# Four attention heads whose probabilities are turned by VectorE and a DRAM round trip and not by TensorE

## The chip, the cores and the metric

The kernel runs on one core of a Trainium2 chip. Its time is the device time of one execution in microseconds; before the change the median of three runs is 907.01 us (906.93 to 907.70). All data are fp32; most matrix products split each fp32 operand into a rounded high part and a rest ("h" and "l") and add three products of the parts.

## The reference

One layer on x of 512 tokens by 1024 features: a SwiGLU feed-forward block, a token mixer, a second feed-forward block and a norm. The mixer has four differential heads (the ones that change here) and eight dilated heads, which the kernel takes in four pairs. For a differential head the reference computes, cut to what matters:

```python
# q, k: two maps (m = 0, 1) of 64 features per head; v: 128 features per head
s = einsum('bhmqd,bhmkd->bhmqk', q, k) * scale + bias      # causal: -inf where k > q
p = softmax(s, axis=-1)
a = p[:, :, 0] - lam * p[:, :, 1]                           # 512 x 512, lower triangle
o = einsum('bhqk,bhkd->bhqd', a, v)
oa = rmsnorm(o, subln_gain) * (1 - lam0)                    # norm over the 128 features of a head
mixed = concatenate([oa, ob]); x = x + mixed @ w_out        # ob: the dilated heads
```

## The kernel before

The mixer is written as a list of chunks for TensorE (PE). Chunk t belongs to step t: function `step` first calls what was `put` at that step with a rank below 10, in order of rank, then the chunk, then what has a rank of 10 and more. PE, VectorE (DVE) and ScalarE (ACT) execute in exactly this written order; the queues that issue DMAs, SyncE's (SP) and GpSimd's, are put in order by the planner of the framework. So a chunk's neighbours on PE, DVE and ACT are known from the numbers in `put`, and DMA issues may be moved among each other.

The chunks are: the projections q and k of units 0 and 1, the values of all units, then eight chunks for q and k of each of the units 2 to 7 (steps 44 to 91, six products of 512 columns a chunk), then the output projection `wo` (from step 92). Units 0 to 3 are the differential heads, 4 to 7 the dilated pairs. A head's attention starts at a step s (41, 49, 57 and 65 for the differential heads): it rides between the projection chunks of later units.

A differential head before the change, `attention(u, s)`:

- `score(m, i)` (L1736 to L1742), one a step from s to s+7: for a block of 128 queries i and map m, two products give up to (i+1) x 128 scores in a PSUM bank (two such banks in turn), DVE adds the bias and takes the row's extreme (L1739), ACT takes the exponential and its sum (L1742). The result lies in the tile `pr` of its map.
- `combine(i)` (L1746 to L1752): DVE joins the two maps, p0 + c p1, in place of p0. Ten blocks of 128 x 128 are left, with queries on the partitions.
- `turn` (L1879, L1881): the value product needs the keys on the partitions. PE turns each of the ten blocks against the identity into a PSUM bank and ACT copies the bank to `ptx`, in three groups of four, two and four blocks.
- `values` (L1891), at s+13: for every block a product with the turned block as stationary operand (128 x 128) and 128 columns of v as moving operand; the framework issues two instructions for each.
- `squares`, `mean`, `scale`, `finish`, `finish_low` (L1897 to L1935), one to seven steps after that: ACT squares with row sums, POOL's power for the norm, `scale` (L1915) in one DVE instruction of 512 columns, four transposes on PE (L1921), ACT and DVE write the two parts `mh` and `ml` that `wo` reads.

The dilated units 5 and 6 already have another way for part of their blocks: `flip` (L1766) turns 32 x 32 squares within a tile on DVE, `away` (L1772) writes the tile to DRAM in four DMAs so that the squares come into place, `back` (L1783) reads it in one DMA, and `values_moved` (L1808) uses it as the moving operand. The tile `tx` holds the turned blocks of all units (one buffer of 3072 columns). Unit 6 turns its other half on PE, `turn_rows` (L1793, L1794).

```python
step, tv = 2 if u else 1, s + 13
put(tv - 2 - step, 2, turn, ((0, 2), (1,)))
put(tv - 2, 2, turn, ((3,),))
put(tv, 1, values)
e = tv + 1
```

Line 188, 189 and 190 are the three products of `mm3`, which the projections, the feed-forward blocks and `wo` use.

Of the kernel before, what the change touches and what calls it, by code (L numbers as in the profile page):

```python
# [28 lines left out]
NQ = S // P  # L29
# [7 lines left out]
WARM = 8  # L37
DIRECT = (7,)
MOVED = {5: (0, 1), 6: (1,)}
PAIRED_ROWS = 5  # L40
BACK = {5: 7, 6: 9}
TAKEN = {5: 16, 6: 13}


# [71 lines left out]
HS = S // 2  # L116
# [11 lines left out]
def tile_macaron(ctx: ExitStack, tc, xs, xT, wf, wgu1, wst1, wdg1, wqk, wvd, wo, wgu2, wst2,  # L128
                 wdg2, fg, lams, relb, addc, xn, out):
    nc = tc.nc  # L130
    V, A, G, T = nc.vector, nc.scalar, nc.gpsimd, nc.tensor
# [4 lines left out]
    tp = ctx.enter_context(tc.tile_pool(name="tp", bufs=2))  # L136
# [3 lines left out]
    dp = ctx.enter_context(tc.tile_pool(name="dp", bufs=1, space=DRAM))  # L140
# [5 lines left out]
    def mm_bank(nm):  # L146
        return pp.tile([P, S], F32, tag="mm", name=nm, bufs=4)
# [10 lines left out]
    x = [None] + [cp.tile([P, S], F32, tag=f"x{k}", name=f"x{k}")[:] for k in range(1, KD)]  # L158
# [930 lines left out]
    with tc.manual_schedule(engines={mybir.EngineType.DVE, mybir.EngineType.Activation}):  # L1089
        for t in range(4):  # L1090
            raw = wp.tile([P, 1024], F32, tag="raw", name=f"raw_f{t}")
            h, l = w_place()
            for kk in range(2):
                k = 2 * t + kk
                c = slice(kk * 512, kk * 512 + 512)
# [282 lines left out]
    start = {w: 8 * i + 20 * (i > 2) for i, w in enumerate(plan)}  # L1378
# [5 lines left out]
    def put(t, rank, f, *a):  # L1384
        at.setdefault(t, []).append((rank, f, a))

    units, chunks = [], []
# [46 lines left out]
    vt = {}  # L1434
# [275 lines left out]
    def attention(u, s):  # L1710
        diff, quick, moved = u < 4, u == 7, u in MOVED
        st = {}
        order = (1, 2, 0, 3) if u >= PAIRED_ROWS else range(NQ)

        def row(m, i):
            w = (i + 1) * P
            if u < PAIRED_ROWS:
                return st["pr"][m][:, OFF[i]:OFF[i] + w]
            o = m * 640 + (0, 0, 2 * P, P)[i]
            return st["pr"][i in (1, 2)][:, o:o + w]  # L1720
# [47 lines left out]
        def away(n):  # L1768
            st["pd", n] = d = dp.tile([4, 32, 4, 320], F32, tag=f"pd{n}", name=f"pd{u}{n}")
            for r in range(4):  # L1770
                part = slice(32 * r, 32 * r + 32)
                nc.sync.dma_start(d[:].rearrange("c j r e -> r j c e")[r],  # L1772
                                           st["tr", n][part, :].rearrange("p (c e) -> p c e", c=4))

        def turned_tx():
            if not shared_tx:
                shared_tx.append(tp.tile([P, 12 * HS], F32, tag="tx", name="ptx_dilated", bufs=1))
            return shared_tx[0]

        def back(n):  # L1780
            o = n * 1280
            st["x", n] = turned_tx()[:, o:o + 1280]
            nc.sync.dma_start(st["x", n], st["pd", n][:].rearrange("c j r e -> (c j) (r e)"))  # L1783

        def turn_rows(part):

            tx = st["x", 0] = turned_tx()[:, :1280]
            pt = pp.tile([P, S], F32, tag="t", name=f"pt{u}{part[0][0]}{part[0][1]}", bufs=2)
            n = 0
            for m, i in part:  # L1790
                o = m * 640 + (0 if i == 0 else P)
                for k in range(i + 1):
                    T.transpose(pt[:, n + k * P:n + (k + 1) * P], row(m, i)[:, k * P:(k + 1) * P], ident[:])  # L1793
                A.copy(tx[:, o:o + (i + 1) * P], pt[:, n:n + (i + 1) * P])  # L1794
                n += (i + 1) * P

        def values_moved():
            po = st["po"] = mm_bank(f"po{u}")
# [19 lines left out]
        def turn_part(m, part):  # L1818


            pt = pp.tile([P, S], F32, tag="t", name=f"pt{u}{m}{part[0][0]}", bufs=2)
            n = 0
            for k, i0, i1 in part:
                for i in range(i0, i1):
                    T.transpose(pt[:, n:n + P], row(m, i)[:, k * P:(k + 1) * P], ident[:])
                    n += P

            if "tx" not in st:
                st["tx"] = turned_tx()
                st["used"] = 0  # L1830
            if quick:

                tx = st["tx"][:, m * KEYS[NQ]:(m + 1) * KEYS[NQ]]
                if part[0][1] == NQ - 1:
                    o = KEYS[1] - P
                    A.copy(tx[:, o:o + 2 * (KEYS[2] - KEYS[1])]
                           .rearrange("p (k q) -> p k q", k=2)[:, :, :P],
                           pt[:, :2 * P].rearrange("p (k q) -> p k q", k=2))
                    A.copy(tx[:, KEYS[NQ] - 2 * P:], pt[:, 2 * P:])
                    return  # L1840
                n = 0
                for k, i0, i1 in part:
# [4 lines left out]
            ptb = st["tx"][:, st["used"]:st["used"] + n]  # L1847
            st["used"] += n
            A.copy(ptb[:, :n], pt[:, :n])
            st["ptb", m, part] = ptb  # L1850

# [17 lines left out]
        def turn(tiles):  # L1869

            if "tx" not in st:
                st["tx"] = tp.tile([P, 12 * HS], F32, tag="tx", name=f"ptx{u}", bufs=1)
            for own in tiles:
                pt = pp.tile([P, S], F32, tag="t", name=f"pt{u}{own[0]}", bufs=2)
                n, c0 = 0, st.get("used", 0)
                for i in own:
                    st["place", i] = c0 + n
                    for k in range(i + 1):
                        T.transpose(pt[:, n:n + P], row(0, i)[:, k * P:(k + 1) * P], ident[:])  # L1879
                        n += P  # L1880
                A.copy(st["tx"][:, c0:c0 + n], pt[:, :n])  # L1881
                st["used"] = c0 + n
# [29 lines left out]
        def scale():  # L1912
            po3, ob = st["po3"], st["ob"]
            V.tensor_tensor(st["f2"], st["f2"], st["y"][:], op=ALU.mult)
            V.tensor_tensor(ob, po3, st["f"][:].to_broadcast([P, NQ, P]), op=ALU.mult)  # L1915

        def finish():
            if diff:
# [24 lines left out]
        step = 1 if quick else 2  # L1943
# [5 lines left out]
                6.5 if (n == 2 if u > 3 and not quick else u == 0 and n == 3) else 5, combine, i)  # L1949
        if diff:  # L1950

            step, tv = 2 if u else 1, s + 13
            put(tv - 2 - step, 2, turn, ((0, 2), (1,)))
            put(tv - 2, 2, turn, ((3,),))
            put(tv, 1, values)
            e = tv + 1
            put(e, 7, squares)
            put(e + 1, 7, mean)
            put(e + 4, 7, scale)
            put(e + 6, 3, finish)  # L1960
            put(e + 7, 8, finish_low)
        elif quick:

            for j, part in enumerate((((0, 0, 3),), ((1, 1, 3), (2, 2, 3)),
                                      tuple((k, 3, 4) for k in range(NQ)))):
                for m in range(2):
                    put(s + 4 + j, 2, turn_part, m, part)
            put(s + 7, 1, values_part, tuple((k, k, NQ) for k in range(NQ)))
            put(s + 7, 3, finish)
            put(s + 7, 4, finish_low)  # L1970
        elif moved:
            put(s + 6, 7, flip, 1)
            put(s + 6, 7.1, away, 1)
            put(s + BACK[u], 2, back, 1)
            if 0 in MOVED[u]:
                put(s + 9 + (u == 4), 9 if u == 4 else 5, flip, 0)
                put(s + 9 + (u == 4), 9.1 if u == 4 else 5.1, away, 0)
                put(s + 11 + (u == 4), 2, back, 0)
            else:
                for n, part in enumerate((((0, 3),), ((1, 3),), ((0, 0), (1, 0)))):  # L1980
                    put(s + 10 + n, 2, turn_rows, part)
            tv = s + TAKEN[u]
            put(tv, 1, values_moved)
            put(tv + 1, 3, finish)
            put(tv + 1, 8, finish_low)
        else:
            tv = s + 9
            parts = ((0, 0, 4),), ((1, 1, 4),), ((2, 2, 4), (3, 3, 4))
            for j, part in enumerate(parts):
                for m in range(2):  # L1990
                    put(tv + j, 2, turn_part, m, part)
                put(tv + 4, 1, values_part, part)
            put(tv + 5, 3, finish)
            put(tv + 5, 8, finish_low)

    for w in plan:
        if w == "V":
# [2 lines left out]
        u = int(w[1])  # L2000
# [10 lines left out]
    def wo_mm(dh, tt, ks):  # L2011
        if (dh, tt) not in wo_ps:
            wo_bank(dh, tt)
        po, c = wo_ps[dh, tt][:], slice(tt * P, (tt + 1) * P)
        for k in ks:
            wh, wl = ready[wo_units[4 * dh + k // 2]]
            o = slice(k % 2 * 512, (k % 2 + 1) * 512)
            mm3(po, mh[k][:, c], ml[k][:, c], wh[:, o], wl[:, o], k == 0, k == KD - 1)

    wo_start = len(chunks)  # L2020
    for kp in range(3):
        chunks += [lambda kp=kp, tt=tt: wo_mm(0, tt, (2 * kp, 2 * kp + 1)) for tt in range(3)]
# [280 lines left out]
```

## Time and profile before

| | |
|---|---|
| median of three runs | 907.01 us |
| profiled execution: its time, and the span of its instructions | 906.15 us, 904.4 us |
| PE busy, weight loads of PE | 894.2 us, 803.6 us |
| DVE, ACT, POOL busy | 752.0 us, 566.2 us, 118.3 us |
| granted clock of PE | 0.999 |
| DMA | 153.05 MB, mean 169 GB/s |

Times below are microseconds from the start of the span. The mixer's attention lies between about 395 and 545. "PEld" are the loads of the stationary operand, which overlap the products ("PE"). The number in square brackets behind an instruction is the time for which its engine had waited, and for whom. A group `out<-in x40` has forty instructions of one kind. The span is 1.75 us shorter than the time of the same execution.

### The profile page before, as it was taken

To read this page: it belongs to the slowest core of one execution; us is meant where nothing else is said; L and a number is where in the kernel's file an instruction comes from. 1 tells how busy PE (TensorE), PEld (TensorE's weight loads), DVE (VectorE), ACT (ScalarE), POOL (GpSimd) and SP (SyncE) were. 2 spreads that over 40 slices of the span, in tenths; PEclk is the share of its full clock that TensorE was granted. 3 is DMA by queue.
4 is the path that set the end of the run, shared out by engine and by line. 5 is a ranking of instruction groups with operands and counts; after the bars stand their busy time and mean duration, and the time that the engine had idled before them with its cause. 6 is when DMAs were issued, how large, how long until landed. Compare 5 with 4: busy or idle time off the path is not lost.

```text
span 904.4 us, 15918 instructions
## 1 busy us (share of the span) xinstructions
PE 894.2 (99%) x5640; PEld 803.6 (89%) x5640; DVE 752.0 (83%) x1519; ACT 566.2 (63%) x1192; POOL 118.3 (13%) x148
## 2 busy tenths in 40 slices
PE   9999999999999999999999999999999999999997
PEld 7888998899998889888888768989999889999885
DVE  7698998889888888887887945888888888988985
ACT  7355666466667766757777665656666546666573
POOL 0101202121122110100000000111112112212200
PEclk9999999999999999999999999999999999999999
DMA  7464869677789663624443713475779679779902
GB/s 259 128 164 121 237 180 241 151 198 185 193 220 276 181 194 84 154 89 141 117 134 99 233 59 117 95 185 138 186 180 247 162 178 247 199 188 237 267 13 93
DMA packets 73903, 153.05 MB, mean 169 GB/s; under 512 B 8480, under 2 KB 10528, under 8 KB 73824
## 3 DMA queue, kind: packets, MB, share of 16 engines
q1 hardware_dynamic: 56240, 119.84, 41.2%
q0 software_dynamic: 17584, 32.20, 21.9%
q8 instruction: 44, 0.72, 0.3%
q14 instruction: 35, 0.29, 0.1%
HBM read 144.24 MB, written 4.10 MB: 164 GB/s over the span
## 4 chain that ended last, share of the span: by engine, by line
PE 94%; DVE 2%; DMA 1%; ACT 1%; issue 1%; SPq 0%; POOLq 0%; DVEq 0%; ACTq 0%
PE pt L188 8%; PE pt L189 8%; PE pt L190 8%; PE pua L188 2%; PE pua L190 2%; PE pua L189 2%; PE pq L188 2%; PE pq L189 1%; PE pk L190 1%; PE pq L190 1%; PE pk L189 1%; PE pk L188 1%; PE pwo L190 1%; PE pwo L188 1%; PE pwo L189 1%; PE pga L188 1%
## 5 line engine op out<-in xcount | busy, mean ns | idle before, releaser
L1742 ACT ACTIVATE pr<-pr,mx 128x128 f32<-128x128 f32 (+3 forms) x64 | 35.9, 562 | 28.4 <-DVE mx L1739 27.3
L544 DVE SCALAR_TENSOR_TENSOR x<-pt,x 128x512 f32<-128x512 f32 x50 | 33.2, 687 | 19.8 <-PE pt L190 12.6
L1739 DVE CUSTOM_DVE_ANT_0 pr<-sc,strip 128x128 f32<-128x128 f32 (+3 forms) x64 | 30.6, 486 | 6.8 <-PE sc L1737 6.0
L450 DVE TENSOR_TENSOR w<-s2b,w 128x512 fp32r<-128x512 f32 x38 | 26.0, 685 | 8.0 <-ACT w L446 8.0
L446 ACT CAST w<-raa 128x512 fp32r<-128x512 f32 x34 | 20.9, 622 | 18.6 <-DVE raa L414 10.3
L446 ACT CAST w<-s2b 128x512 fp32r<-128x512 f32 x38 | 23.6, 620 | 6.3 <-DVE s2b L419 6.3
L446 ACT CAST w<-rab 128x512 fp32r<-128x512 f32 x28 | 17.1, 622 | 16.3 <-DVE rab L414 7.5
L188 PE MATMUL pwo<-w,mh 128*128 128x512 f32 x64 | 25.9, 405 | 0.2 <-ACT mh L1929 0.2
L190 PE MATMUL pwo<-w,ml 128*128 128x512 f32 x64 | 25.1, 393 | 0.5 <-DVE ml L1938 0.5
L189 PE MATMUL pwo<-w,mh 128*128 128x512 f32 x64 | 25.0, 390 | 0.0
L450 DVE TENSOR_TENSOR w<-s2a,w 128x512 fp32r<-128x512 f32 x30 | 20.5, 684 | 3.0 <-ACT w L446 2.8
L446 ACT CAST w<-s2a 128x512 fp32r<-128x512 f32 x30 | 18.6, 621 | 6.6 <-DVE s2a L419 5.8
L1736 PE MATMUL sc<-k,q 128*128 128x128 f32 (+3 forms) x64 | 21.9, 343 | 0.8 <-DVE mx L1739 0.8
L450 DVE TENSOR_TENSOR w<-raa,w 128x512 fp32r<-128x512 f32 x34 | 22.6, 683 | 0.0
L189 PE MATMUL pxgb<-ttb,w 128*128 128x256 f32 x80 | 22.5, 281 | 0.0
L221 POOL TENSOR_TENSOR fin<-fin,half 128x1 f32<-128x1 f32 (+1 forms) x7 | 4.0, 568 | 137.3 <-DVE fin L1286 85.7
L389 POOL DMA_DIRECT2D s1bg<-wst_dram x10 | 8.7, 873 | 92.8 <-DVE w L450 38.8
L1737 PE MATMUL sc<-l,q 128*128 128x128 f32 (+3 forms) x64 | 20.4, 320 | 0.0
L189 PE MATMUL pxub<-ttb,w 128*128 128x256 f32 x72 | 20.2, 281 | 0.0
L389 POOL DMA_DIRECT2D s1ag<-wst_dram x8 | 7.1, 888 | 94.8 <-DMA s1ag<-wst_dram 32.9
L1416 DVE TENSOR_TENSOR w<-raw_qk,w 128x512 fp32r<-128x512 f32 x24 | 16.5, 688 | 3.6 <-ACT w L1412 3.5
L221 POOL TENSOR_TENSOR yi<-ss,half 128x4 f32<-128x4 f32 x4 | 4.1, 1015 | 113.0 <-DVE ss L1908 113.0
(1176 smaller groups left out, 3932.2 us busy)
## 6 DMA issues: line engine op xcount, KB each, us to landing
raw_qk<-wqk_dram SPq DMA_DIRECT2D x12, 512.0 KB, 3.5
raw0bg<-wst_dram SPq DMA_DIRECT2D x10, 512.0 KB, 5.4
raw0bu<-wst_dram SPq DMA_DIRECT2D x9, 512.0 KB, 5.7
raw_gua<-wgu_dram SPq DMA_DIRECT2D x8, 512.0 KB, 3.6
raw0ag<-wst_dram SPq DMA_DIRECT2D x8, 512.0 KB, 4.9
strip<-bias_rows SPq DMA_DIRECT2D x16, 256.0 KB, 3.7
raw_wo<-wo_dram SPq DMA_DIRECT2D x8, 512.0 KB, 3.5
raw0au<-wst_dram SPq DMA_DIRECT2D x7, 512.0 KB, 5.9
```

The source lines that it names most:

```text
L188: T.matmul(po, wh, mh, start=first, stop=False, skip_group_check=on)
L189: T.matmul(po, wh, ml, start=False, stop=False, skip_group_check=on)
L190: T.matmul(po, wl, mh, start=False, stop=last, skip_group_check=on)
L389: nc.gpsimd.dma_start(t[:], b, accum_op=ALU.add)
L446: A.copy(made[t][0], source(t))
L450: V.tensor_tensor(l, source(t), h.bitcast(F32), op=ALU.subtract)
L544: V.scalar_tensor_tensor(o, a, f, b, op0=ALU.mult, op1=op1)
L1416: V.tensor_tensor(l[:, c:c + 512], raw[:, c:c + 512], h[:, c:c + 512].bitcast(F32), op=ALU.subtract)
L1736: T.matmul(ps[:, :w], qs[:, qi], ks[:, :w], start=True, stop=False)
L1737: T.matmul(ps[:, :w], qs[:, qi], ls[:, :w], start=False, stop=True)
L1739: V.tensor_tensor_reduce(out=pi, in0=ps[:, :w], in1=st["b"][m][:, w - 1::-1], op0=ALU.add, op1=ALU.min, scale=1.0, scalar=3.0e38, accum_ou ...
L1742: A.activation(pi, pi, AF.Exp, scale=-1.0, bias=st["mx"][:, m, i:i + 1], accum_out=st["ls"][:, m, i:i + 1])
```

## The change

Differential heads are no longer turned on PE. For each, the head's ten blocks are put in two halves of five (blocks of queries 1 and 2: n = 1; of 0 and 3: n = 0), and for each half:

- `diff_flip`: one DVE transpose of 32 x 32 squares over 128 x 640, from the first map's `pr` into the second map's `pr` (no longer needed there), written so that the five blocks of a half lie interleaved: element a of block b at a * 5 + b, a step of five words.
- `diff_away`: four DMAs to DRAM, in pieces of 160 words (640 bytes).
- `diff_back`: one DMA into `tx`, 2560 bytes a partition. Two regions of `tx` serve the heads in turn.

`diff_values` then reads block b + k as stationary operand with `b + k:640:5`. It comes at s+21 and not s+13; what follows it moves by as much, with `scale` one step earlier and on ACT, as four instructions with a scale per query, in place of the one on DVE. Query blocks now come in the order 1, 2, 0, 3. Because the last differential head now reaches into the dilated units, unit 4 turns and uses its values one or two steps later and at fixed places of `tx`, unit 5's first `back` comes a step later, unit 6's two single blocks are turned first and copied together, and the output projection takes unit 5's part after unit 4's in all three token blocks.

```diff
+MOVED_DIFF = (0, 1, 2, 3)
+DIFF_FLIP = (11, 7)
+DIFF_BACK = (16, 12)
+DIFF_TAKEN = 21
+PART_PLACES = {(0, 0): 0, (1, 0): 2560, (0, 1): 512, (1, 1): 896, (0, 2): 1280, (1, 2): 1664}
-BACK = {5: 7, 6: 9}
+BACK = {5: 8, 6: 9}
...
-        order = (1, 2, 0, 3) if u >= PAIRED_ROWS else range(NQ)
+        order = (1, 2, 0, 3) if u >= PAIRED_ROWS or u in MOVED_DIFF else range(NQ)
...
+            if u in MOVED_DIFF:
+                o = (5 * P, 0, 2 * P, 6 * P)[i]
+                return st["pr"][m][:, o:o + w]
...
+        def diff_flip(n):
+            o = (1 - n) * 640
+            t = st["tr", n] = st["pr"][1][:, o:o + 640]
+            V.transpose(t.rearrange("p (c a b) -> p b c a", c=4, b=5), st["pr"][0][:, o:o + 640])
+
+        def diff_away(n):
+            st["pd", n] = d = dp.tile([4, 32, 4, 160], F32, tag=f"pe{n}", name=f"pe{u}{n}")
+            for r in range(4):
+                nc.sync.dma_start(d[:].rearrange("c j r e -> r j c e")[r],
+                                  st["tr", n][32 * r:32 * r + 32, :].rearrange("p (c e) -> p c e", c=4))
+
+        def diff_back(n):
+            o = u % 2 * 1280 + n * 640
+            st["x", n] = turned_tx()[:, o:o + 640]
+            nc.sync.dma_start(st["x", n], st["pd", n][:].rearrange("c j r e -> (c j) (r e)"))
+
+        def diff_values():
...
+            for i, n, b in ((1, 1, 0), (2, 1, 2), (0, 0, 0), (3, 0, 1)):
+                for k in range(i + 1):
+                    T.matmul(st["po3"][:, i, :], st["x", n][:, b + k:640:5], vt[0, k][:, fo:fo + P],
+                             start=k == 0, stop=k == i)
...
-                A.copy(tx[:, o:o + (i + 1) * P], pt[:, n:n + (i + 1) * P])
                 n += (i + 1) * P
+            if len(part) > 1:
+                A.copy(tx.rearrange("p (m e) -> p m e", m=2)[:, :, :P], pt[:, :n].rearrange("p (m q) -> p m q", m=2))
+            else:
+                A.copy(tx[:, o:o + n], pt[:, :n])
...
-            V.tensor_tensor(ob, po3, st["f"][:].to_broadcast([P, NQ, P]), op=ALU.mult)
+            for i in range(NQ):
+                A.activation(ob[:, i, :], po3[:, i, :], AF.Copy, scale=st["f2"][:, i:i + 1])
...
-            step, tv = 2 if u else 1, s + 13
-            put(tv - 2 - step, 2, turn, ((0, 2), (1,)))
-            put(tv - 2, 2, turn, ((3,),))
-            put(tv, 1, values)
+            step, tv = 2 if u else 1, s + (DIFF_TAKEN if u in MOVED_DIFF else 13)
+            if u in MOVED_DIFF:
+                for n in range(2):
+                    put(s + DIFF_FLIP[n], 9.2, diff_flip, n)
+                    put(s + DIFF_FLIP[n], 9.3, diff_away, n)
+                    put(s + DIFF_BACK[n], 2, diff_back, n)
+                put(tv, 1, diff_values)
...
-            put(e + 4, 7, scale)
-            put(e + 6, 3, finish)
-            put(e + 7, 8, finish_low)
+            put(e + 3, 5, scale)
+            put(e + 6 - (u == 3), 3, finish)
+            put(e + 7 - (u > 1), 8 if u < 3 else 1, finish_low)
...
-                for n, part in enumerate((((0, 3),), ((1, 3),), ((0, 0), (1, 0)))):
+                for n, part in enumerate((((0, 0), (1, 0)), ((0, 3),), ((1, 3),))):
...
-                put(tv + 4, 1, values_part, part)
-            put(tv + 5, 3, finish)
-            put(tv + 5, 8, finish_low)
+                    put(tv + j + late * (1 + (j == 2)) // 2, 2, turn_part, m, part)
+                put(tv + 4 + late, 1, values_part, part)
+            put(tv + 5 + late, 3, finish)
+            put(tv + 5 + late, 8, finish_low)
...
-        chunks += [lambda kp=kp, tt=tt: wo_mm(0, tt, (2 * kp, 2 * kp + 1)) for tt in range(3)]
+        chunks += [lambda kp=kp, tt=tt: wo_mm(0, tt, (2 * kp, 2 * kp + 1)) for tt in range(3)] if kp < 2 else [
+        lambda part=part: [wo_mm(0, tt, (k,)) for k, tt in part]
+        for part in (((4, 0), (4, 1)), ((4, 2), (5, 0)), ((5, 1), (5, 2)))]
```

Left out are lines that give `turn` and `turn_part` their fixed places in `tx` and the `else` branch that keeps the old way. `late` is 2 for unit 4 and 0 otherwise.

More of the change, by code (lines that the diff above doesn't have):

```diff
@@ L1773, in away @@
                                            st["tr", n][part, :].rearrange("p (c e) -> p c e", c=4))
+        def diff_flip(n):
[12 more added lines that the diff above has]
+        def diff_values():
+            st["po"] = mm_bank(f"po{u}")
+            st["po3"] = st["po"][:].rearrange("p (i d) -> p i d", i=NQ)
+            fo = (u % 4) * P
+            for i, n, b in ((1, 1, 0), (2, 1, 2), (0, 0, 0), (3, 0, 1)):
+                for k in range(i + 1):
+                    T.matmul(st["po3"][:, i, :], st["x", n][:, b + k:640:5], vt[0, k][:, fo:fo + P],
+                             start=k == 0, stop=k == i)
         def turned_tx():
@@ L1829, in turn_part @@
                 st["tx"] = turned_tx()
-                st["used"] = 0
             if quick:
@@ L1846, in turn_part @@
                 return
-            ptb = st["tx"][:, st["used"]:st["used"] + n]
-            st["used"] += n
+            o = PART_PLACES[m, part[0][0]]
+            ptb = st["tx"][:, o:o + n]
             A.copy(ptb[:, :n], pt[:, :n])
@@ L1871, in turn @@
             if "tx" not in st:
-                st["tx"] = tp.tile([P, 12 * HS], F32, tag="tx", name=f"ptx{u}", bufs=1)
+                st["tx"] = turned_tx()[:, u % 2 * 1280:(u % 2 + 1) * 1280]
             for own in tiles:
@@ L1950, in attention @@
         if diff:
-            step, tv = 2 if u else 1, s + 13
-            put(tv - 2 - step, 2, turn, ((0, 2), (1,)))
-            put(tv - 2, 2, turn, ((3,),))
-            put(tv, 1, values)
+            step, tv = 2 if u else 1, s + (DIFF_TAKEN if u in MOVED_DIFF else 13)
[5 more added lines that the diff above has]
+                put(tv, 1, diff_values)
+            else:
+                put(tv - 2 - step, 2, turn, ((0, 2), (1,)))
+                put(tv - 2, 2, turn, ((3,),))
+                put(tv, 1, values)
             e = tv + 1
@@ L1987, in attention @@
             tv = s + 9
+            late = 2 * (u == 4)
             parts = ((0, 0, 4),), ((1, 1, 4),), ((2, 2, 4), (3, 3, 4))
@@ L1990, in attention @@
                 for m in range(2):
-                    put(tv + j, 2, turn_part, m, part)
-                put(tv + 4, 1, values_part, part)
-            put(tv + 5, 3, finish)
-            put(tv + 5, 8, finish_low)
+                    put(tv + j + late * (1 + (j == 2)) // 2, 2, turn_part, m, part)
+                put(tv + 4 + late, 1, values_part, part)
+            put(tv + 5 + late, 3, finish)
+            put(tv + 5 + late, 8, finish_low)
     for w in plan:
```

## The prediction

> **What bounds the kernel now.** I read the page's busy times and its chain first, then the stretches of one differential head each, then the chain of waits between 395 and 545, where the change lies.
>
> ```profile
> PE 894.2 (99%) x5640; PEld 803.6 (89%) x5640; DVE 752.0 (83%) x1519; ACT 566.2 (63%) x1192; POOL 118.3 (13%) x148
> ...
> PE 94%; DVE 2%; DMA 1%; ACT 1%; issue 1%; SPq 0%; POOLq 0%; DVEq 0%; ACTq 0%
> ```
>
> PE is busy for 99% of the span and is 94% of the chain that ended last: an instruction taken from PE shortens the end, as long as nobody else becomes late. The heads themselves:
>
> ```profile
> core 0: us, PE busy (x) PEld busy (x) DVE busy (x) ACT busy (x) POOL busy (x), PEclk, DMA share, GB/s
> 439.46:456.75 17.29, 17.29 (x100) 14.99 (x98) 14.37 (x43) 12.78 (x37) 1.01 (x1) 1.00 0.42 122
> 456.75:474.04 17.29, 17.29 (x100) 15.00 (x99) 14.29 (x43) 12.78 (x37) 1.01 (x1) 1.00 0.46 123
> ```
>
> A head takes 17.29 and PE never pauses in it, at a granted clock of 1.00. DVE has 2.9 free, ACT 4.5. So PE is the bound by a margin that DVE's additions could use up.
>
> **PE: what goes.** In the chain of waits in order of time (start, us, engine, tile, line) the turning of a head on PE stands as two pieces:
>
> ```profile
> 416.11 0.66 PE pt L1879 x6
> 418.38 0.44 PE pt L1879 x4
> ...
> 439.62 2.23 PE po L1891 x20
> ...
> 466.10 0.66 PE pt L1879 x6
> ```
>
> 0.66 + 0.44 = 1.10 a head, 4.4 for four. The timeline agrees: with four transposes ahead, a score pair of 256 columns takes 0.67 until the next projection (452.54 to 453.21), without them 0.23 (450.92 to 451.15).
>
> **PE: what stays, but is read otherwise.** The twenty value instructions of a head keep their shape; their stationary operand is now read with a step of five words. They start 2.15/20 = 0.107 apart (456.75 to 458.90).
>
> ```profile
> L1891 PEld LDWEIGHTS po<-v,ptx x80: 186/192/192, 422.1 to 476.0; 128*128 128x128 f32 x80
> ...
> L1808 PEld LDWEIGHTS po<-ptx_dilated,v x56: 133/137/137, 514.2 to 530.5; 128*64 128x64 f32 x56
> ...
> L1879 PEld LDWEIGHTS pt<-ident,pr x40: 138/140/143, 415.7 to 470.0; 128*128 128x128 f32 x40
> ```
>
> Loads of 128 columns last about 54 ns longer than loads of 64 (187 against 133), so a column costs 0.84 ns and a load streams for 108 ns: the same as the spacing. Hence there is no slack: whatever a load grows by, the eighty value instructions grow by. No load in this trace has a step. The low end is no change (a step can't speed up the reading of as many words). For the high end: the loads of transposes bring 128 columns in some 60 ns (140 less the 80 that the other two rows leave as fixed part), so between the rows the same count differs by 1.8; I take a factor of two, +8.6 in all. I take no change, since of the rows the value load itself is nearest, and since the fast loads show that it does not run at the limit of what is read.
>
> [...]
>
> **DVE and ACT.**
>
> ```profile
> L1766 DVE STREAM_TRANSPOSE tr<-pr x6: 793/817/839, 498.0 to 513.9; 128x640 f32<-128x640 f32 x6
> ...
> L1915 DVE TENSOR_TENSOR ob<-po,f x4: 691/691/692, 434.6 to 487.6; 128x512 f32<-128x512 f32 x4
> ...
> L1881 ACT COPY ptx<-pt x12: 377/586/587, 416.6 to 470.5; 128x512 f32<-128x512 f32 x8, 128x256 f32<-128x256 f32 x4
> ...
> L1899 ACT ACTIVATE ob<-po,cs x16: 347/359/370, 428.4 to 481.3; 128x128 f32<-128x128 f32 x16
> ```
>
> DVE gets two flips a head, 1.63 by the existing flip, which writes runs of 32 words where the new one writes single words with a step of five. It loses the 0.69 of `scale`. So 14.37 + 0.94 = 15.31 in a head of 17.29 - 1.10 = 16.19: 95%, covered, but barely. Part of the cover is DVE's own waiting at the very steps at which the flips stand (s+7 and s+11):
>
> ```profile
> 448.52 0.69 DVE L1416 TENSOR_TENSOR w<-raw_qk,w 128x512 fp32r<-128x512 f32 x1 [0.52 <-ACT w L1412]
> ...
> 454.87 1.41 DVE L1188 TENSOR_TENSOR l<-pk,k 64x512 fp32r<-64x512 f32 x2 [1.03 <-ACT k L1185]
> ```
>
> Without cover a flip delays the release of a score bank, and PE waits. A flip can't be cheaper than the 0.82 of the same op with longer runs; for the dear end I take twice it, 1.63. I choose 0.82, the nearest row; the end far off is rival C. ACT loses 2 x 0.586 + 0.377 = 1.55 a head and gains four scales, 4 x 0.359 = 1.44 by the squares of the same shape: nothing.
>
> [...]
>
> **DMA and the SP queue.**
>
> ```profile
> L1772 SPq DMA_DIRECT2D pd<-tr x12: 302/435/584, 499.6 to 516.0; - x12
> ...
> DMA to landing us min/median/max: 2.1/3.6/5.2
> ...
> L1783 SPq DMA_DIRECT2D ptx_dilated<-pd x3: 319/337/338, 505.5 to 518.9; - x3
> ...
> DMA to landing us min/median/max: 3.8/5.0/5.1
> ...
> L1640 SPq DMA_DIRECT2D k<-k x14: 467/498/540, 376.3 to 490.6; - x14
> ```
>
> A head issues eight aways and two backs, 8 x 0.435 + 2 x 0.337 = 4.2 of SP's 16. A step is 17.29 / 8 = 2.2. From an away's step to its back's are five steps, 10.8, against 0.8 for the flip, 1.7 for four issues and at most 5.2 to land; from the last back to the values again five steps against 5.1. Both are covered; if the back came 5 later, PE would wait. Behind an away on SP, while it waits for its flip, stand the next 512 KB load of weights, two strips and the halves of k (L1640). The halves are read five steps later, so a delay of 0.8 + 1.7 is hidden there; the weights are rival D.
>
> **The other edits.** At the seam with `wo` PE waits in four places:
>
> ```profile
> 515.87 1.31 PE L1808 MATMUL po<-ptx_dilated,v 128*64 128x256 f32 x16 [0.35 <-DMA ptx_dilated<-pd]
> ...
> 520.90 0.39 PE L190 MATMUL pwo<-w,ml 128*128 128x512 f32 x1
> 521.50 0.50 PE L188 MATMUL pwo<-w,mh 128*128 128x512 f32 x1 [0.22 <-ACT mh L1929]
> 521.84 0.40 PE L189 MATMUL pwo<-w,mh 128*128 128x512 f32 x1
> 522.70 0.50 PE L190 MATMUL pwo<-w,ml 128*128 128x512 f32 x1 [0.46 <-DVE ml L1938]
> ...
> 525.92 0.33 PE L1793 MATMUL pt<-ident,pr 128*128 128x128 f32 x1 [0.36 <-ACT ptx_dilated L1794]
> ```
>
> Products of 512 columns follow each other after 0.23 where nothing waits. Here it is 0.60 and 0.86, so 0.37 + 0.63 = 1.0 is lost, because unit 5's part is wanted as soon as it is made. The new order puts nine products of unit 4 (2.0) and a pair of scores ahead of it: -1.0. Unit 6's two single blocks, turned together and copied once, save the wait of 0.36: -0.4. Against that stands the wait at 515.87 for unit 5's `back`. Its chain runs from the score of step 88 over DVE and ACT; the squares of the last differential head (4 x 0.559 = 2.2 with their reads) now come at step 87 ahead of it on ACT, which idles there for about as long. Between 0 and +2.2; I take +0.4, since most of it finds idle time. The rest (order of query blocks, places in `tx`, `finish` of the last head) issues the same instructions at other steps, where PE runs on; at nothing, with PE's work as the cover.
>
> **Sum.** -4.4 - 1.0 - 0.4 + 0.4 = -5.4. The profiled execution, 906.15 with a span of 904.4, becomes 900.75 (span 899.0). The median stands 0.86 above that execution, so the predicted median is 907.01 - 5.4 = **901.6**, with 900 to 904 as the forecast's own range.
>
> **Rivals.**
>
> *B, slower: the stepped load.* If the load of 128 single words takes twice as long, the values of a head go from 2.15 to 4.3, and the change costs 8.6 - 5.4 = +3.2: 910.2. It decides from 1.63 times the load on (5.4 / 8.6), that is from about 175 ns of streaming. For it: spacing and load are equal, so nothing hides it. Against it: 60 ns loads exist.
>
> *C, DVE becomes the bound.* At 1.63 a flip, DVE has 14.37 - 0.69 + 3.27 = 16.95 a head against PE's 16.19: 0.76 x 4 = 3.0 of the gain goes back, 904.6; with 0.4 of unavoidable waiting for ACT a head the whole 4.4 does, 906. I put it at 905.2. For it: DVE's 95%. Against it: DVE's waits of 0.5 to 1.0 are the first to vanish when it is late.
>
> *D, the SP queue.* If the weights' load stands behind an away, it is issued after the flip and not 2 ahead of its step, and lands some 0.8 + 1.7 + 3.5 to 6.0 into a stretch of four steps (8.6) at whose end ACT wants it. One such miss of 0.5 to 1 a head: 904. Against it: the planner may put the load first.
>
> **Chances.** Forecast 0.56, B 0.24, C 0.12, D 0.08. About 0.2% (1.8) is what a measurement here tells from no change, so faster is below 905.2. All of the forecast and about a quarter of C and half of D lie there: 0.56 + 0.03 + 0.03 = 0.62. Slower is B, 0.24; the rest, 0.14, is the same. The range from 899.6 to 910.5 holds the forecast, C, D and the larger part of B.
>
> **What would show it.** In the changed profile: no transposes of the differential heads on PE and a head of about 16.2; value instructions 0.107 apart and a load of 187 to 192 (B: well above, a PE stretch of 4 a head); flips at 0.82 (C: near 1.6, with scores waiting for DVE's `mx`); no wait of PE or ACT for `tx` or raw weights (D); the two waits of `wo` gone. The prediction is wrong if the load grows by more than half.

## The result and the profile after

The changed kernel takes 913.12 us (912.74 to 914.53, six runs) against 906.83 of the kernel before beside it: ratio 1.0073, interval 1.006 to 1.0086. It is slower by 6.3 by the medians (6.6 by the ratio), where 5.4 less was forecast. Its profiled execution has a span of 911.2 against 904.4, so 6.8 is what the two traces have to explain, and in both the granted clock is 0.999.

First the page's busy times and its chain, of the kernel after:

```profile
PE 897.7 (99%) x5600; PEld 808.2 (89%) x5600; DVE 758.3 (83%) x1523; ACT 564.6 (62%) x1195; POOL 118.5 (13%) x148
...
PE 94%; DVE 3%; DMA 1%; ACT 1%; issue 0%; SPq 0%; POOLq 0%; DVEq 0%; ACTq 0%
```

PE has forty instructions less, and is busy for 3.5 longer. So something that stayed on PE has become longer. Below are the groups of the value products' loads, of the products, and of the flips (least, median and largest ns of one; first and last start):

```profile
L1805 PEld LDWEIGHTS po<-v,ptx_dilated x80: 294/317/321, 436.9 to 498.6; 128*128 128x128 f32 x80
L1805 PE MATMUL po<-v,ptx_dilated x80: 271/386/457, 436.9 to 498.7; 128*128 128x128 f32 x80
...
L1786 DVE STREAM_TRANSPOSE pr<-pr x8: 1383/1419/1460, 413.1 to 471.7; 128x640 f32<-128x640 f32 x8
```

The load of 128 words with a step of five takes 317 ns, the packed one took 186 to 192. The flip takes 1.42 and not 0.82. What the load does to a head is seen in the chain, in order of time, where the twenty value instructions of a head stood with 2.23 to 2.40 before:

```profile
436.92 4.70 PE po L1805 x20
...
456.11 4.68 PE po L1805 x20
...
474.63 4.43 PE po L1805 x20
...
494.74 4.35 PE po L1805 x20
...
508.73 0.49 ACT mh L1965
509.24 0.69 DVE ml L1974
...
510.60 1.48 DVE tr L1774 x2
...
514.37 6.30 DMA pd<-tr
520.75 3.92 DMA ptx_dilated<-pd
```

And what PE waited for between 395 and 560 (us in total, times, the longest):

```profile
PE sc L1744 <- DVE mx L1747: 2.2, 2, 1.3
PE po L1844 <- DMA ptx_dilated<-pd: 2.0, 1, 2.0
PE po L1805 <- issue: 1.4, 2, 0.9
```

The same view of before had one wait of the scores:

```profile
PE sc L1736 <- DVE mx L1739: 0.8, 1, 0.8
```

It had 0.35 for unit 5's read, none for the values, and 0.4, 0.5 and 0.2 for the transposes of unit 6 and the two of `wo`, which are gone. The scores' two waits after the change, with the first flip of the kernel between them:

```profile
407.47 0.33 PE L1744 MATMUL sc<-k,q 128*128 128x128 f32 x1 [1.27 <-DVE mx L1747]
...
413.05 1.46 DVE L1786 STREAM_TRANSPOSE pr<-pr 128x640 f32<-128x640 f32 x1
...
425.63 0.50 PE L1744 MATMUL sc<-k,q 128*128 128x512 f32 x1 [0.97 <-DVE mx L1747]
```

So the first of them, 0.5 longer than the one before, is not the flip's doing. What differs ahead of it is the order of the query blocks; no run tests that alone. The account, from before to after: transposes -4.4; the seam's waits, 0.36 + 0.37 + 0.63, -1.4; values 18.16 - 9.09 = +9.1; scores 2.2 - 0.8 = +1.4; values' waits +1.4; unit 5's read 2.04 - 0.35 = +1.7. That is +7.8 against the measured 6.8. Of the 1.0 between them, 0.45 lies ahead of the change: the first score of the first head, behind the same work on PE, starts at 397.75 and not at 398.20. The other half isn't found, so such an account closes to about half a microsecond.

Two stretches, the one ahead of the first head's values and the one from the second head's values to the third's, with DVE's load (us, then busy time and count of PE, PEld, DVE, ACT, POOL; clock; DMA share; GB/s):

```profile
417.00:436.90 19.90, 18.06 (x85) 14.56 (x84) 19.33 (x50) 13.35 (x33) 0.00 (x0) 1.00 0.56 159
...
456.11:474.60 18.49, 18.49 (x89) 16.23 (x90) 15.48 (x44) 12.12 (x38) 1.01 (x1) 1.00 0.57 159
```

In the second stretch PE never pauses, at a clock of 1.00, and yet it takes 18.49: the 17.29 of before, less 1.10 for the transposes, plus about 2.3 for the values. In the first one DVE is busy for 97%, and PE pauses for 1.84: the scores' second wait of 0.97 and one of 0.89 ahead of the values.

### The profile page after: what moved, and what is told of

It is laid out like the page before. It is cut to its first block, busy times and chain, and to the rows that moved or that the text cites. A ratio compares the mean times of both kernels' runs of the same rounds, so it can differ in the third digit from the quotient of the medians.

```text
span 911.2 us, 15897 instructions
## 1 busy us (share of the span) xinstructions
PE 897.7 (99%) x5600; PEld 808.2 (89%) x5600; DVE 758.3 (83%) x1523; ACT 564.6 (62%) x1195; POOL 118.5 (13%) x148
## 4 chain that ended last, share of the span: by engine, by line
PE 94%; DVE 3%; DMA 1%; ACT 1%; issue 0%; SPq 0%; POOLq 0%; DVEq 0%; ACTq 0%
PE pt L195 8%; PE pt L193 8%; PE pt L194 8%; PE po L1805 2%; PE pua L193 2%; PE pua L195 2%; PE pua L194 2%; PE pwo L193 1%; PE pwo L195 1%; PE pwo L194 1%; PE pq L193 1%; PE pq L194 1%; PE pk L193 1%; PE pq L195 1%; PE pk L194 1%; PE pk L195 1%
## 5 line engine op out<-in xcount | busy, mean ns | idle before, releaser
L1750 ACT ACTIVATE pr<-pr,mx 128x256 f32<-128x256 f32 (+3 forms) x64 | 36.0, 562 | 38.8 <-DVE mx L1747 37.5
L1747 DVE CUSTOM_DVE_ANT_0 pr<-sc,strip 128x256 f32<-128x256 f32 (+3 forms) x64 | 30.7, 487 | 14.1 <-PE sc L1745 13.8
L1744 PE MATMUL sc<-k,q 128*128 128x256 f32 (+3 forms) x64 | 21.1, 331 | 2.2 <-DVE mx L1747 2.2
L1745 PE MATMUL sc<-l,q 128*128 128x256 f32 (+3 forms) x64 | 20.4, 321 | 0.0
L1805 PEld LDWEIGHTS po<-v,ptx_dilated 128*128 128x128 f32 x80 | 18.1, 316 | 2.3 <-issue 2.2
L1805 PE MATMUL po<-v,ptx_dilated 128*128 128x128 f32 x80 | 18.5, 386 | 1.4 <-issue 1.4
```

Of the source, the lines that this page charges most:

```text
L1744: T.matmul(ps[:, :w], qs[:, qi], ks[:, :w], start=True, stop=False)
L1745: T.matmul(ps[:, :w], qs[:, qi], ls[:, :w], start=False, stop=True)
L1747: V.tensor_tensor_reduce(out=pi, in0=ps[:, :w], in1=st["b"][m][:, w - 1::-1], op0=ALU.add, op1=ALU.min, scale=1.0, scalar=3.0e38, accum_ou ...
L1750: A.activation(pi, pi, AF.Exp, scale=-1.0, bias=st["mx"][:, m, i:i + 1], accum_out=st["ls"][:, m, i:i + 1])
L1805: T.matmul(st["po3"][:, i, :], st["x", n][:, b + k:640:5], vt[0, k][:, fo:fo + P], start=k == 0, stop=k == i)
```

## Experiments

### One change at a time: the load

The value products read 128 neighbouring words of `tx` in place of 128 with a step of five; all else is as after the change.

```diff
-    T.matmul(..., st["x", n][:, b + k:640:5], ...)
+    T.matmul(..., st["x", n][:, (b + k) * 120 + 20:(b + k) * 120 + 20 + P], ...)
```

> The changed kernel, but the values read 128 neighbouring words of the turned tile as stationary operand, not every fifth (other elements, so the output isn't the reference's; same number and shape of instructions, flips and DMAs as in the changed kernel). Theory (the stepped load is the loss): a load back at 187 ns, twenty value instructions in 2.2 us and not 4.5, so 913.1 - 9.1 = 904.0, between 903 and 905.5. Rival (VectorE's dear flips or late DMAs are the loss and PE would wait there anyway): 910 to 913.

```profile
L1805 PEld LDWEIGHTS po<-v,ptx_dilated x80: 186/192/192, 437.5 to 490.8; 128*128 128x128 f32 x80
...
PE sc L1744 <- DVE mx L1747: 2.2, 2, 1.3
PE po L1844 <- DMA ptx_dilated<-pd: 2.1, 1, 2.1
PE po L1805 <- issue: 1.4, 2, 0.9
```

905.34, ratio 0.9986 (0.9977 to 0.9996), span 903.6. The step alone is worth 7.8 of the median and 7.6 of the span (8.2 counted from the first head's first score, which starts at 398.34 here and at 397.75 in the changed kernel); the waits, which have to do with DVE and the DMAs, stand as they were. With the same account (-4.4 - 1.4 + 1.4 + 1.4 + 1.75, and +0.5 for values of 2.23 to 2.47) the span would be 904.4 - 0.75 = 903.65, as measured. So even with a load that costs nothing extra the change would have gained 1.3 and not 5.4; the rest of the miss lies in the waits.

### The step in the kernel before, alone

No part of the change but the step: the kernel before reads words of its tile of turned blocks with a step of five (other words than it needs, so that only the time counts).

```diff
-                    T.matmul(st["po3"][:, i, :], st["tx"][:, o:o + P],
+                    T.matmul(st["po3"][:, i, :], st["tx"][:, 33 + 61 * (i + k):33 + 61 * (i + k) + 127 * (5, 5, 5, 5)[u] + 1:(5, 5, 5, 5)[u]],
```

> The kernel before, with its transposes on TensorE, copies and times of the values, but the values read the turned tile with a step of five words as stationary operand (other elements, so the output isn't the reference's). Theory (the step itself makes the load dear, whoever wrote the tile): loads 317 ns, values of a head 4.5 and not 2.2, time +9.1 to 915.8, between 914.5 and 917. Rival (the load is dear because DMA wrote the tile or because of its place): loads 187, time as before.

```profile
L1891 PEld LDWEIGHTS po<-v,ptx x80: 296/316/318, 422.1 to 484.5; 128*128 128x128 f32 x80
```

914.70, ratio 1.0094 (1.0079 to 1.0109), span 913.1 against 904.4. The twenty value instructions of a head take 4.60, 4.32, 4.32 and 4.32 in the chain, 17.56 - 9.09 = 8.5 of the 8.7. In this kernel no flip and no DMA writes what these loads read, and they are as slow: so neither of the two is the cause. The forecast's high end for this term was 8.6.

### Which step costs what

The four heads of the kernel before read with steps of 2, 3, 4 and 8 words.

```diff
-                    T.matmul(st["po3"][:, i, :], st["tx"][:, o:o + P],
+                    T.matmul(st["po3"][:, i, :], st["tx"][:, 17 + 13 * (i + k):17 + 13 * (i + k) + 127 * (2, 3, 4, 8)[u] + 1:(2, 3, 4, 8)[u]],
```

> The kernel before, the four heads' values read with steps of 2, 3, 4 and 8 words (other elements, output isn't the reference's). [...] If neighbouring pairs of words count, as the dear flip suggests for VectorE: already step 2 at 317. If the load grows with the distance: 2 < 3 < 4 < 8.

Its one execution took 911.96. The loads, a row for each head in this order:

```profile
L1891 PEld LDWEIGHTS po<-v,ptx x20: 193/198/201, 421.7 to 424.0; 128*128 128x128 f32 x20
L1891 PEld LDWEIGHTS po<-v,ptx x20: 250/263/266, 439.1 to 442.4; 128*128 128x128 f32 x20
L1891 PEld LDWEIGHTS po<-v,ptx x20: 308/330/332, 457.6 to 462.0; 128*128 128x128 f32 x20
L1891 PEld LDWEIGHTS po<-v,ptx x20: 316/334/337, 477.2 to 481.7; 128*128 128x128 f32 x20
```

From 2 to 3 and from 3 to 4 the load grows by 65 and 67 ns, from 4 to 8 by 4, and step five (316) lies with these. What grows and then stops is the number of 16-byte pieces that 128 words touch: 64, 96, 128, and 128 from a step of four on. Less the 79 fixed ns that follow from the prediction's two load rows, that is 119, 184, 251, 237 (step five) and 255 ns, or 1.85 to 2.0 ns a piece; a packed load touches 32 pieces, and its 108 to 113 fit the 0.84 ns a column of the same two rows. Step two, at 64 pieces, is just on the boundary between the two. Its 198 is also far from the 317 expected if only neighbouring pairs of words counted, and the 4 ns from step 4 to 8 speak against the distance.

With one word of a piece read the load takes 2.2 times the streaming time of a packed one (237 ns against 108), with two words 1.1 times (119). The columns alone don't set it: with the five steps, loads of 128 columns took 198 to 334 ns. That pieces of 16 bytes are what counts is inferred from these five steps; no view names them. The loads of transposes, 140 ns for 128 columns (61 without the fixed part), don't fit the 0.84 a column, and why they are shorter was not shown.

### The flip

The flip writes runs of 32 words, as unit 5's and 6's flips do; the load keeps its step, over words in another order.

```diff
-    V.transpose(t.rearrange("p (c a b) -> p b c a", c=4, b=5), ...)
+    V.transpose(t.rearrange("p (c b a) -> p b c a", c=4, b=5), ...)
```

> The changed kernel, but the flip writes runs of 32 words and not single words with a step of five; the values still read with a step of five (other elements, output isn't the reference's). Theory: flips from 1.42 to 0.82 us, the two waits of scores for VectorE (1.27 and 0.97) and part of unit 5's wait (2.04) go, 913.1 - 2 = 911, between 910 and 912.5, with loads still at 317 ns. Rival (VectorE is the bound of a head): 8 x 0.6 = 4.8 less or more, 908 or below.

```profile
L1786 DVE STREAM_TRANSPOSE pr<-pr x8: 839/840/843, 413.5 to 469.9; 128x640 f32<-128x640 f32 x8
...
PE sc L1744 <- DVE mx L1747: 1.7, 2, 1.3
PE po L1844 <- DMA ptx_dilated<-pd: 1.6, 1, 1.6
PE po L1805 <- issue: 0.2, 1, 0.2
```

911.96, ratio 1.0057 (1.0042 to 1.0072), span 909.1. The same 640 columns take 0.84 in runs of 32 and 1.42 as single words: 1.3 against 2.2 ns a column. 8 x 0.58 = 4.6 of DVE's time gives the span 2.1: 1.2 of the values' wait, 0.5 of the scores' and 0.4 of unit 5's read. By the medians it is 1.2 only; the profiled execution was the shortest of the four. The values' wait, then, comes from DVE. Ahead of the values at 436.92 DVE ran a flip from 434.16 and two subtractions of k's rest, `l<-pk,k`, until 436.82 in the changed kernel; here the subtractions end at 435.99 and the values start at 436.10, and ahead of the second head's values, at 456.11 in the changed kernel, they end at 456.01. Three times PE starts 0.1 behind them. That it waited for the bank in PSUM that they free is inferred from this, no view names it.

### The reads from DRAM a step earlier

```diff
-DIFF_BACK = (16, 12)
+DIFF_BACK = (15, 12)
```

> The changed kernel with DIFF_BACK = (15, 12): the second half's way back stands a step earlier, so ahead of the next head's first away in SyncE's queue. Theory (the back waits in the queue behind an away that waits for its flip): the waits of 0.89 and 0.47 ahead of the first two heads' values go, 913.1 - 1.4 = 911.7. Rival (the landing itself is slow): nothing changes.

914.40, ratio 1.0094 (1.0079 to 1.0109), span 912.5; waits 2.2, 2.2 and 1.3 in the order of the fence above. The values wait as long with their data earlier (the second head's second read leaves at 442.91 and not at 450.54), as the rival had it. So the wait was not for the read, and the prediction's count of five steps for each way stands.

### The seam alone

Only the new order of the `wo` products and unit 6's two blocks copied together, in the kernel before.

```diff
-    chunks += [lambda kp=kp, tt=tt: wo_mm(0, tt, (2 * kp, 2 * kp + 1)) for tt in range(3)]
+    ... if kp < 2 else [lambda part=part: [wo_mm(0, tt, (k,)) for k, tt in part]
+    for part in (((4, 0), (4, 1)), ((4, 2), (5, 0)), ((5, 1), (5, 2)))]
...
```

Left out are the lines on unit 6, which are those of the change.

> The kernel before with only two edits: the output projection takes unit 5's part after unit 4's in three token blocks, and unit 6's two single blocks are turned together and copied once. Theory: the waits of 0.22, 0.46 and 0.36 us go, time -1.4, 905.5. Rival: the waits move to the next place, within 0.3 of before.

904.78, ratio 0.9981 (0.9972 to 0.999), span 902.5: -1.9 for these two, where -1.4 was forecast. Of the rest, 0.35 is unit 5's read, for which PE doesn't wait here. So the 2.0 that PE waits for it in the changed kernel does not come from these two edits alone. The chain above shows what is new ahead of that read: unit 4's parts `mh` and `ml`, which the change moved two steps later, stand between unit 5's score and its flip (from DVE's start on the score to the flip 4.35, before 3.18), and the away takes 6.30 to land. Before it took:

```profile
506.85 4.47 DMA pd<-tr
```

No run separates the two.

### A packed load for the price of smaller DMA pieces

The flip writes runs of 32 words, and the read from DRAM puts the blocks in place: four DMAs a half, in pieces of 128 bytes. Then load and flip both see neighbouring words.

```diff
-    V.transpose(t.rearrange("p (c a b) -> p b c a", c=4, b=5), ...)
+    V.transpose(t.rearrange("p (c b a) -> p b c a", c=4, b=5), ...)
...
-    nc.sync.dma_start(st["x", n], st["pd", n][:].rearrange("c j r e -> (c j) (r e)"))
+    for r in range(4):
+        nc.sync.dma_start(st["x", n].rearrange("p (b r a) -> p r b a", b=5, r=4)[:, r],
+                          st["pd", n][:, :, r, :].rearrange("c j (b a) -> (c j) b a", b=5))
...
-    T.matmul(..., st["x", n][:, b + k:640:5], ...)
+    T.matmul(..., st["x", n][:, (b + k) * P:(b + k + 1) * P], ...)
```

> Flip writes runs of 32 words, and the way back is four DMAs a half, each putting pieces of 128 bytes where they belong, so that every block lies packed and the values read 128 neighbouring words; result as the reference's. Theory: both costs of the step go, 913.1 - 9.1 - 2 = 902, between 900.5 and 904, if the small pieces land within the five steps (about 10.8 us) that they have. Rival (the DMA can't carry 128-byte pieces in time): landing above 11 us, PE waits before each values group by what is over, 906 or more.

```profile
L1798 SPq DMA_DIRECT2D ptx_dilated<-pe x32: 388/580/3213, 418.3 to 482.3; - x32
...
DVE pr L1747 <- DMA strip<-bias_rows: 6.8, 3, 2.8
...
PE sc L1744 <- DVE mx L1747: 3.4, 4, 1.3
PE po L1846 <- DMA ptx_dilated<-pd: 1.4, 1, 1.4
PE pt L1863 <- ACT ptx_dilated L1886: 1.1, 1, 1.1
PE po L1807 <- issue: 0.7, 2, 0.4
```

908.01, ratio 1.0018 (1.0008 to 1.0027), span 906.6. Loads are back at 192 ns, yet the gain is gone: 32 issues of 0.58 on SP, one of 3.2, and four scores and a transpose that wait. On DVE there are three waits for the strips of bias, which SP issues behind these reads; neither the kernel before nor the changed one has them. Rival D, work standing in SP's queue, shows here for the first time. The test is the same kernel with these reads on GpSimd's queue (and issued one step earlier):

```diff
-        nc.sync.dma_start(st["x", n].rearrange(...)[:, r], ...)
+        nc.gpsimd.dma_start(st["x", n].rearrange(...)[:, r], ...)
```

> As the run with pieces of 128 bytes sorted on the way back, but those DMAs are issued by GpSimd's queue and the second half's a step earlier; result as the reference's. Theory (in that run SyncE's longer queue delayed weights and strips, and so VectorE and scores): the waits of 0.85, 0.84 and 1.13 go, 908.0 - 3 - 0.7 = 904.3. Rival (small pieces are slow to land or GpSimd is slow to issue them): PE waits ahead of the values, 908 or more.

902.92, ratio 0.996 (0.9946 to 0.9974): now faster than before, and DVE's waits for strips are gone. GpSimd needs 0.87 an issue, but behind these stands only the power for the norm. Two things were changed, the queue and the step; an earlier step alone had gained nothing in the changed kernel, so the gain is put down to the queue. In the profiled execution one large wait was left, the 2.8 for unit 5's read, and the products behind it ran slower. The next runs are on that place.

### Unit 5's read and the clock

The kernel of the last run, with unit 5's values one step later:

```diff
-TAKEN = {5: 16, 6: 13}
+TAKEN = {5: 17, 6: 13}
```

> The kernel with blocks placed by the read from DRAM, issued by GpSimd's queue, and in it unit 5's values one step later (step 17 of the unit and not 16); nothing else differs. In the profiled execution without this edit PE waited 2.81 for unit 5's last block to land, and then ran at a granted clock of 0.50 to 0.56 for 6.4 us. Theory: the wait comes from the chain score, flip, away, back, which has one step too few at the seam, so a step more (about 2 us of products) covers most of it: wait below 1, clock 1.00 after it, time 899 to 902. Rival: products of the output projection need unit 5's part a step later too, so the wait turns up again at the output projection in another name (PE waiting for ACT's or DVE's parts of unit 5): time 902 to 904, no gain over the same kernel without this edit.

In this kernel the values come behind the first `wo` products that take unit 5's part, so those read what its place held before; the amount of work is the same. 912.74, ratio 1.007 (1.0057 to 1.0084). The timeline of PE, where the bracket is the wait:

```profile
515.10 0.55 PE L1744 MATMUL sc<-k,q 128*128 128x256 f32 x1 [3.78 <-DVE rl L1754]
...
522.25 4.53 PE L1846 MATMUL po<-ptx_dilated,v 128*64 128x256 f32 x28 [3.83 <-DMA ptx_dilated<-pd]
```

Neither theory nor rival had this: the values, moved away, had filled the time in which the next pair of scores waits for DVE, and PE now waits twice. So unit 5's values can't go later at this place. That landing earlier than about 514 would gain little is argued from the first wait, not tested.

Next the kernel as it was (values at step 16), once more, beside one in which two loads of 512 KB for `wo` come four steps later:

```diff
-    put(wo_start, 0, load, wo_units[3])
-    put(wo_start + 2, 0, load, wo_units[4])
+    put(wo_start + 4, 0, load, wo_units[3])
+    put(wo_start + 6, 0, load, wo_units[4])
```

> The kernel with blocks placed by the read from DRAM, issued by GpSimd's queue, once more, beside the version with later weights on the same chip: 902 to 904. Its profiled execution was the slowest of its five (905.94 with a wait of PE of 2.81 for unit 5's read and a granted clock of 0.50 to 0.56 behind it). Theory: the low clock follows only from a long wait, so an execution with a shorter wait shows clock 1.00 and about 902.5. Rival: the low clock comes with this place in every execution, and the profiled execution is then again 3 above the median.

> The kernel with blocks placed by the read from DRAM, issued by GpSimd's queue, and in it the two loads of 512 KB for the output projection's third and fourth weight unit four steps later, so that the first of them stands behind unit 5's last read from DRAM on SP and not ahead of it; the result is as the reference's. In the profiled execution without this edit that read (320 KB) was issued 1.6 us behind a load of 512 KB and 2.7 us behind a strip of 256 KB, took 6.7 us to land where its median is 4.9, and PE waited 2.81, after which its granted clock was 0.50 to 0.56 for 6.4 us. Theory: the read shares the DMA engines with the weights' 512 KB, so without them ahead it lands in about 5 us: wait about 1, clock 1.00 after it, time 900 to 902. Rival: what is late is the chain before it (score, flip, away) and the strip, so the wait stays at 2 or more and the time at 902 to 904; or the weights come late and PE, ACT or DVE waits for raw weights after step 100.

The unchanged one took 904.66, ratio 0.9974 (0.9963 to 0.9984). Its profiled execution and the earlier one have the same wait (2.84 and 2.81) and spans of 901.5 and 904.2. The stretches about the wait's end, first of the earlier execution (514.66), then of the later one (515.03):

```profile
514.60:518.00 3.40, 3.34 (x20) 2.63 (x21) 1.42 (x8) 1.54 (x3) 0.00 (x0) 0.50 0.83 246
518.00:521.00 3.00, 3.00 (x11) 2.31 (x11) 1.20 (x6) 1.09 (x4) 0.00 (x0) 0.56 0.60 217
```

```profile
514.00:516.00 2.00, 0.97 (x14) 0.82 (x16) 1.68 (x7) 1.11 (x3) 0.00 (x0) 1.00 0.86 254
516.00:518.00 2.00, 2.00 (x18) 1.63 (x13) 1.29 (x6) 1.44 (x4) 0.00 (x0) 1.00 0.77 240
```

So the low clock comes behind this wait, but not in every execution. Where it comes, it costs 3.0: from PE's start behind the wait to the end of the span are 389.5 in the one and 386.5 in the other. Of the nine executions of the later run, five have a mean clock of 0.997 and a median of 905.07, four 0.999 and 903.13. The rival that it comes each time is out.

The later weights made it worse: 908.10, ratio 1.0013 (1.0004 to 1.0022). SP's queue and PE in that kernel:

```profile
512.07 0.30 SPq L1780 DMA_DIRECT2D pd<-tr  x1
512.54 0.34 SPq L1818 DMA_DIRECT2D ptx_dilated<-pd  x1
```

```profile
517.38 2.40 PE L1846 MATMUL po<-ptx_dilated,v 128*64 128x256 f32 x16 [5.35 <-DMA ptx_dilated<-pd]
```

The planner, with the weights moved, put an away that waits for its flip at 512 ahead of the read; SP stood still from 505.9 to 512.07, and the read left about four later than it could. PE waited 5.35, and the clock was at 0.50 from 516 to 522. Theory and rival both missed this; it is rival D's mechanism with other work held up. The last run keeps the later weights and gives unit 5's two reads to GpSimd's queue.

```diff
-    nc.sync.dma_start(st["x", n], ...)
+    (nc.gpsimd if u == 5 else nc.sync).dma_start(st["x", n], ...)
```

> The version with the weights of the output projection loaded four steps later, and in it unit 5's two reads from DRAM issued by GpSimd's queue and not by SP's; the result is as the reference's. With the later weights alone the read was issued at 512.54 and not at 508, since SP's list had an away of the next half, which waits for its flip at 512, ahead of it; PE waited 5.35. Theory: with a queue of its own the read is issued at about 508 again as soon as the aways have landed, and with no 512 KB ahead of it lands in 4 to 5 us: wait of PE 0 to 1.5, clock 1.00 throughout, time 899.5 to 902. Rival: the later weights cost elsewhere (a wait of ACT or DVE for raw weights, about 1 each), time 902 to 904; or the landing stays above 6 because the strip's 256 KB alone slows it, wait 2.5 or more, time 903 to 905.

```profile
508.05 0.54 POOL L1818 DMA_DIRECT2D ptx_dilated<-pd  x1 [7.50 <-DMA pd<-tr]
```

```profile
PE sc L1744 <- DVE mx L1747: 1.7, 2, 1.3
PE po L1846 <- DMA ptx_dilated<-pd: 1.2, 1, 1.2
PE po L1807 <- issue: 0.2, 1, 0.2
```

902.46, ratio 0.9957 (0.9943 to 0.9972), a wait of 1.2 and a clock of 1.00 behind it, as the theory had it; the time lies 0.5 above its range. The read leaves as soon as the aways have landed. A load of weights still stands ahead of it (SP issued one at 506.29), and it took 5.8 to land, so what the weights cost the read was not tested. This version's profiled span, 900.7, is accounted for: -4.4 - 1.4 + 0.9 (scores) + 0.9 (unit 5) + 0.2 = -3.8 of the measured -3.7. Its time is the lowest of the study and below both kernels; from the version without its two last edits (902.92 and 904.66 in two runs) it can't be told apart.

## Why the prediction was wrong

The step that failed is the choice "I take no change" for the stepped load. It was priced between 0 and +8.6, and measured +8.5 alone and +9.1 in the changed kernel. Rival B had named the mechanism, its price of 4.3 a head (measured 4.35 to 4.70) and the point from which it decides (1.63 times the streaming; measured 2.2 times). Two reasons had been given for "no change", and both were about packed loads. The row of the value load was called nearest, but it touches 32 pieces of 16 bytes and the new load 128. And the 60 ns loads of transposes show that packed words can come faster, not that single words can. No row was about steps, so neither end of the price had been measured.

B's total of 910.2 came out too low because three more terms were mis-sized:

- The flip, chosen at 0.82 with the dear end at 1.63, took 1.42. Rival C's mechanism came with it, in part: the run with flips of 0.84 had 2.1 less of waits, where C's first price was 3.0.
- Unit 5's read, chosen at +0.4 of 0 to +2.2, took +1.7. The squares on ACT that the prediction gave as the reason are not in the chain: they end at 504.79, and ACT then waits 2.12 for DVE. In the chain stand unit 4's later parts and an away that lands in 6.30 (4.47 before). Which of them delays the read, and why the away lands late, stays open.
- The order of the query blocks, put at nothing. The scores' first wait, ahead of the first flip, grew from 0.76 to 1.27, and it is 1.3 in every run with the new order.

What held: the transposes gone from PE, -4.4, with which the account of the packed load closes; the two waits of `wo` and unit 6's wait, all gone (-1.4); nothing for ACT (564.6 against 566.2); the heads' reads in time, as the earlier read shows. Rival D did not touch the changed kernel, but decided the version with smaller pieces.

## What to carry to other kernels

A layout that suits the transfer can cost the engine that writes it and the one that reads it: 1.42 us and 317 ns here both come from a step of five words, and moving the same reordering into the DMA read took the price off DVE and PE (0.84 us and 192 ns). When no row tests a price, a row that looks near is not enough; count what each touches (here pieces of 16 bytes, 32 against 128) before calling a row near. DMA issues that wait belong on a queue where nothing urgent stands behind them: the same reads took the kernel to 908.01 on SP's queue and to 902.92 on GpSimd's.

## What the runs showed of the hardware

- A stationary operand of fp32 words: about 1.9 ns per 16-byte piece touched, or 0.84 ns a column, whichever is longer, on top of 79, fits the value loads measured here; step two is nearly free (198 ns against 192), three costs 263, four, five and eight 316 to 334. The 140 ns of the transposes' loads it doesn't fit.
- Behind a wait of PE of 2.8 the granted clock was 0.50 in one of two profiled executions, from about a microsecond before PE resumed and for some 6 after it, at a cost of 3.0; in the other it stayed at 1.00. Waits of 2.0 and 1.2 left it at 1.00; waits of 3.8 and 5.35 were followed by 0.50 too. What decides between the two outcomes of one wait was not shown.
- A flip that stores single words takes 1.42 for 640 columns, in runs of 32 words 0.84.
